# Encoder layer (gated DeltaNet and short convolution) in fp32: roots on GpSimd, merge copies kept on one engine, the second norm scaled ahead of a plain transposition, queries without the learned tokens

## The chip, the cores and the metric

The kernel runs on one core of a Trainium2 chip. The metric is the device time of one execution in microseconds, the median of several runs. Each profile is of one execution. The engines are called as the profile calls them: PE is TensorE (PEld its weight loads), DVE is VectorE, ACT is ScalarE, POOL is GpSimd, and SP is the engine that issues most of the DMAs.

## The reference

One encoder layer works on 1024 rows of 1024 columns with 16 learned tokens ahead of them. Cut to what matters:

```python
h = rmsnorm(h_res, norm1_w)                     # x * rsqrt(mean(x*x) + 1e-6) * w
q, k, v, z, b_raw, a_raw, sc_b, sc_c, sc_x, gate_a, gate_b = split(h @ w_in)
# branch A, 8 heads of 128: centred convolution of q|k|v over 5 rows, SiLU, l2norm of q and k,
#   gated delta rule in chunks of 64 rows, forward and backward, o = o_fwd + o_bwd
#   per chunk: triangular solve with (I + strict lower part of beta * k k^T * decay)
#   o = o * rsqrt(mean(o*o) + 1e-6) * norm_w * silu(z)
# branch B: sc_b * convolution over 3 rows of (sc_c * sc_x)
merged = sigmoid(gate_a) * (o_dn @ w_branch_dn) + sigmoid(gate_b) * (y_b @ w_branch_sc)
h_res += merged @ w_out
gu = rmsnorm(h_res, norm2_w) @ w_gate_up        # 1024 x 5632
h_res += (silu(gu[:, :2816]) * gu[:, 2816:]) @ w_down
out = rmsnorm(h_res, final_norm_w)[16:]
```

All of it is float32. The rows of the learned tokens matter for k, v and the gates, since later rows attend to them; the output leaves these rows out.

## The kernel before

**Products.** Every large product is split for precision: each operand into a high part in the matmul format fp32r and a low part that is the rest, and three matmuls add up (high by high, low by high, high by low: lines 293, 294 and 295 in stage 1, 1269 to 1271 in the output projection, 1329 to 1331 in part two). A split is a cast on ACT and a subtraction on DVE (lines 86 and 87, 889 and 886, 988 and 991).

**Start (0 to 23 us).** Nine row tiles, the first with the 16 learned tokens ahead, come in groups of 1, 2, 3 and 3 (loop at line 948). ACT squares a tile and sums it (L957). DVE makes 1/rms of the whole group: a mean (L958), then `rsqrt` (L127 to L141), an integer shift and a magic constant for a first guess, and three Newton steps. L979 multiplies a tile by 1/rms and by the weight row w1row, PE transposes it (L83), and L988 and L991 split it. POOL sets up masks and identities meanwhile, lines 1020 to 1051. Here the compiler's scheduler sets the order of each engine.

**Stage 1 (23 to 1057 us).** PE works through dense units: for each of the 8 heads k, q and v (`u_qkv`, i = 0, 1, 2), and the short convolution's and the gates' columns. A unit has three chunks of columns (QCH: 336, 320 and 384 of the 1040 rows) of 24 matmuls each. Heads are worked on between them, each as a stream: `g_norm` (squares, k by k, the decayed matrices PQ and NP), `g_inv` (the inverse of the triangular matrix, by blocks of 16 merged to 32, 64 and 128), and `g_scan` (the chunked recurrence, then the norm of o and its transposition). The order is written by hand: each stream is a generator that yields a due time, clocks T for pe, dve, act and pool are moved on by `on`, `pe`, `A` and `V` with planned costs, and whichever is due goes next, with dense matmuls as filling. Jobs for DVE (`conv_job`, `norm_job`, `norm`) are queued in lanes and taken one instruction at a time. An engine keeps strictly to the order in which this plan emits. POOL carries the decay tables of the next heads on short rows (L609 to L619), some of which wait for a DMA.

**Merges.** In `g_inv`, the step from 32 to 64 multiplies small blocks into two PSUM banks, pp and px (L672 to L674). Four blocks of pp go to NP by copies on ACT and DVE in turn (L679 and L676), then one block of px to X64 on each (L681 on DVE, L682 on ACT); X64 is part of the tile XT. The next matmuls (L689, L690) read both. The step from 64 to 128 copies one half on ACT (L699) and one on DVE (L700).

**Norm of o.** `g_scan` ends with a job on DVE: the root of nine columns, then eight instructions that scale one chunk of o each; after it PE transposes four chunks at a time.

**Second norm (1300 to 1412 us).** The output projection goes row tile by row tile. DVE adds the residual (L1272) and multiplies by the weight row (L1277), ACT squares (L146), DVE makes 1/rms (L147, L126 to L135). One tile later `norm_T` makes diag(1/rms) (L158) and lets PE multiply the tile by it, in full fp32 (L166, eight products of 128 by 128), which scales and transposes together. The last tile's norm_T comes behind the first product of part two. The scheduler sets the order.

**Part two and the tail (1412 to 2032 us).** The gate and up columns go through a Strassen scheme, then the down projection adds into rows; `finish` scales a row tile by the final norm (L1489 to L1497). Of the last four tiles half is squared ahead of time; when the last half has come, it is squared (L1490), joined (L1491), the root is taken (L126 to L135), and both halves are scaled on ACT (L1494) and DVE (L1496) and stored.

Of the kernel before, what the change touches and what calls it, by code (L numbers as in the profile page):

```python
# [10 lines left out]
I32 = mybir.dt.int32  # L11
# [26 lines left out]
def encoder_layer(ctx: ExitStack, tc: tile.TileContext, x, meta, norm1_w, w_in,  # L38
# [84 lines left out]
    def rsqrt(y, a, tmp):  # L123
        column = y.shape[-1] == 1
        if column:
            nc.vector.tensor_scalar(out=tmp, in0=a, scalar1=-0.5, scalar2=None, op0=ALU.mult)  # L126
        nc.vector.tensor_scalar(out=y.bitcast(I32), in0=a.bitcast(I32), scalar1=1, scalar2=None,  # L127
                                op0=ALU.logical_shift_right)
        nc.vector.tensor_scalar(out=y.bitcast(I32), in0=y.bitcast(I32), scalar1=-1,
                                scalar2=0x5F3759DF, op0=ALU.mult, op1=ALU.add)  # L130
        if column:

            for _ in range(3):
                nc.vector.scalar_tensor_tensor(out=a, in0=y, scalar=tmp, in1=y, op0=ALU.mult, op1=ALU.mult)
                nc.vector.scalar_tensor_tensor(out=y, in0=a, scalar=1.5, in1=y, op0=ALU.add, op1=ALU.mult)  # L135
            return
        for _ in range(3):
            nc.vector.tensor_tensor(out=tmp, in0=y, in1=y, op=ALU.mult)
            nc.vector.scalar_tensor_tensor(out=tmp, in0=tmp, scalar=-0.5, in1=a,
                                           op0=ALU.mult, op1=ALU.mult)  # L140
            nc.vector.scalar_tensor_tensor(out=y, in0=tmp, scalar=1.5, in1=y,  # L141
                                           op0=ALU.add, op1=ALU.mult)

    def rms_scale(pool, src, p, tag, junk):
        ss = pool.tile([P, 3], F32, tag=tag, name=uid(tag), bufs=3)
        nc.scalar.activation(junk[:p], src, AF.Square, accum_out=ss[:p, 0:1])  # L146
        nc.vector.tensor_scalar(out=ss[:p, 0:1], in0=ss[:p, 0:1], scalar1=1.0 / D, scalar2=EPS,  # L147
                                op0=ALU.mult, op1=ALU.add)
        rsqrt(ss[:p, 1:2], ss[:p, 0:1], ss[:p, 2:3])
        return ss[:p, 1:2]  # L150
# [4 lines left out]
    def norm_T(t, rs, hn):  # L155

        diag = tp.tile([P, P], F32, tag="diag", name=uid("diag"), bufs=1)
        nc.vector.tensor_scalar(out=diag, in0=ident, scalar1=rs, scalar2=None, op0=ALU.mult)  # L158
        c = slice(t % 4 * P, t % 4 * P + P)
        pts = []  # L160
        for g in range(2):
            pt = psany().rearrange("p (k t) -> p k t", k=4)
            pts.append(pt)
            for k in range(4):
                kk = 4 * g + k
                mm(pt[:, k], hn[:, kk * P:(kk + 1) * P], diag, start=True, stop=True)  # L166
# [47 lines left out]
    QCH = ((0, 336), (336, 320), (656, 384))  # L214

# [93 lines left out]
    def conv_job(raw, dst, col, st_, key):  # L309

        for h0, hn in HALF:
# [16 lines left out]
    def u_qkv(h, i, w):  # L328
# [9 lines left out]
        for ci, (t0, n) in enumerate(QCH):  # L338
            po = psm()
            yield from dense_steps(po, w, hx, t0, n)  # L340
            if raw is None:
                raw = row_buffer()
                nc.gpsimd.memset(raw[:, 0:2], 0.0)
# [6 lines left out]
            if ci == 1:  # L350
                job = enqueue("conv", conv_job(raw, dst, col, sub, "t"))
                raws.append(job)
# [103 lines left out]
    def norm_job(st_, ssk1, cc, ce, he, y, tmp, sk):  # L456
        nc.vector.tensor_tensor(out=ce, in0=cc, in1=he, op=ALU.mult)
        V(18)
        yield T["dve"] + DEP
        rsqrt(y, ssk1, tmp)  # L460
        [V(9) for _ in range(11)]
# [28 lines left out]
    def g_norm(h, st_):  # L490
# [5 lines left out]
        ssk, ssq, rk2, ssk1, y, tmp, sk = (small[:, :, i] for i in range(7))  # L496
# [51 lines left out]
        nc.vector.tensor_scalar(out=ssk1, in0=ssk, scalar1=EPS, scalar2=None, op0=ALU.add)  # L548
        nc.vector.reciprocal(rk2, ssk1)
# [4 lines left out]
        on("dve", 500)  # L554
# [20 lines left out]
        enqueue("norm", norm_job(st_, ssk1, cc, ce, he, y, tmp, sk))  # L575

    def g_inv(h, st_):
# [96 lines left out]
        for i, (d, a, b, Xs, xo) in enumerate(pairs):  # L674
            if i % 2:
# [878 lines left out]
```

## Time and profile before

| | us |
|---|---|
| three runs | 2034.18, 2039.75, 2039.87 |
| median | 2039.75 |
| the profiled execution, its own time | 2033.3 |
| its span | 2031.6 |
| ACT busy in the span | 791.9 |

The span is the stretch from the first to the last instruction of the core, and 1.7 us of the execution lie around it. A row of a timeline gives the start in us, the duration, the engine, the line, the operation, what it writes and reads, the shape, how many instructions in a row it stands for, and in brackets how long the engine was idle just before and what ended that. A row of windows gives the stretch, its length, and for PE, PEld, DVE, ACT and POOL the busy time with the number of instructions, then PE's granted clock, the busy share of the DMA engines and GB/s. A row of the waits has the waiting line, the line that released it, and the total, the number and the longest of the waits.

### The profile page before, as it was taken

Reading aid. Unit: us, or ns where it says so; the run is one execution under the profiler, and the core shown is the slowest. Engines: PE = TensorE matmul, PEld = TensorE weight load, DVE = VectorE, ACT = ScalarE, POOL = GpSimd, SP = SyncE. Lnnn points to the kernel's source line nnn. Section 1 sums busy time; section 2 is a strip of 40 time slices with the busy share of each in tenths; the row PEclk is TensorE's granted clock in tenths of the full one; section 3 lists DMA queues with packets and bytes.
Section 4 is the critical chain, followed back from the end, with each engine's and each line's share of the span. In section 5 each row is a group of like instructions: output and inputs, shape, how many; then the busy total and the mean of one; then the engine's idle time right before and its main releaser. Section 6 shows DMA issues by size and latency. Waiting matters only on the chain.

```text
span 2031.6 us, 32113 instructions
## 1 busy us (share of the span) xinstructions
PE 1982.7 (98%) x12075; PEld 1732.7 (85%) x12075; DVE 1412.6 (70%) x3129; ACT 791.9 (39%) x1873; POOL 108.0 (5%) x394
## 2 busy tenths in 40 slices
PE   6999999999999999999999999999999999999998
PEld 6899998999999888988888888888888888878886
DVE  6789586887887797857245534458988777756576
ACT  5363235364544554453334211124323222224343
POOL 1002110202020201101000000000000000000000
PEclk9999999999999999999999999999999999999999
DMA  4122322222222223232327743122766345477654
GB/s 141 39 88 68 74 60 63 78 63 57 75 58 84 59 79 84 71 92 79 99 63 233 233 135 115 52 98 84 254 225 220 129 167 172 159 267 248 195 176 156
DMA packets 250723, 248.40 MB, mean 122 GB/s; under 512 B 46085, under 2 KB 190774, under 8 KB 248134
## 3 DMA queue, kind: packets, MB, share of 16 engines
q1 hardware_dynamic: 250565, 246.34, 38.9%
q8 instruction: 95, 1.56, 0.3%
q14 instruction: 63, 0.51, 0.1%
HBM read 179.62 MB, written 66.67 MB: 121 GB/s over the span
## 4 chain that ended last, share of the span: by engine, by line
PE 80%; DVE 11%; ACT 3%; DMA 2%; issue 1%; SPq 0%; POOL 0%; DVEq 0%; ACTq 0%; POOLq 0%
PE pm L293 9%; PE pm L295 9%; PE pm L294 9%; PE pm L1330 3%; PE pm L1331 3%; PE pm L1329 3%; PE pd L1330 2%; PE pd L1331 2%; PE pd L1329 2%; DVE kq L316 2%; PE pe L1331 2%; PE pe L1330 2%; PE pe L1329 2%; PE pd L121 1%; PE pd L120 1%
## 5 line engine op out<-in xcount | busy, mean ns | idle before, releaser
L293 PE MATMUL pm<-hTh,wh 128*128 128x384 f32 (+4 forms) x1424 | 525.9, 369 | 3.5 <-issue 1.3
L295 PE MATMUL pm<-hTh,wl 128*128 128x384 f32 (+4 forms) x1424 | 490.4, 344 | 0.4 <-issue 0.2
L294 PE MATMUL pm<-al,wh 128*128 128x384 f32 (+4 forms) x1424 | 488.8, 343 | 0.3 <-DVE al L991 0.3
L295 PEld LDWEIGHTS pm<-hTh,wl 128*128 128x128 f32 x1424 | 267.6, 188 | 20.6 <-issue 0.5
L293 PEld LDWEIGHTS pm<-hTh,wh 128*128 128x128 f32 x1424 | 268.8, 189 | 19.2 <-ACT wh L889 1.4
L294 PEld LDWEIGHTS pm<-al,wh 128*128 128x128 f32 x1424 | 269.0, 189 | 17.1 <-issue 1.4
L87 DVE TENSOR_TENSOR al<-raw,ring_h 128x1024 fp32r<-128x1024 f32 x73 | 88.5, 1223 | 65.3 <-ACT ring_h L86 64.7
L886 DVE TENSOR_TENSOR wl<-raw,wh 128x512 fp32r<-128x512 f32 x134 | 90.6, 688 | 52.9 <-ACT wh L889 52.5
L86 ACT CAST ring_h<-raw 128x1024 fp32r<-128x1024 f32 x73 | 76.7, 1054 | 106.3 <-PE pe L1474 37.5
L316 DVE SCALAR_TENSOR_TENSOR kq<-ra,wc,kq 128x520 f32<-128x520 f32 x128 | 97.3, 760 | 3.8 <-ACT kq L346 2.4
L86 ACT CAST wh<-raw 128x1024 fp32r<-128x1024 f32 x45 | 47.4, 1053 | 122.8 <-issue 30.0
L771 ACT ACTIVATE w<-pd,small 128x128 f32<-128x128 f32 x128 | 40.1, 365 | 111.0 <-PE pd L764 102.7
L889 ACT CAST wh<-raw 128x512 fp32r<-128x512 f32 x134 | 78.7, 618 | 9.7 <-PE pm L294 9.6
L452 DVE TENSOR_TENSOR fP<-fP,tm 128x135 f32<-128x135 f32 (+23 forms) x248 | 71.4, 288 | 5.0
L448 DVE TENSOR_TENSOR tm<-fP,fN 128x135 f32<-128x135 f32 (+23 forms) x248 | 71.5, 288 | 4.3
L1333 DVE TENSOR_TENSOR b<-pm,b 128x512 f32<-128x512 f32 x67 | 45.1, 687 | 33.2 <-PE pm L1331 31.0
L793 DVE SCALAR_TENSOR_TENSOR S<-S,eGl,pd 128x128 f32<-128x128 f32 x104 | 31.8, 344 | 49.7 <-PE pd L781 26.6
L87 DVE TENSOR_TENSOR wl<-raw,wh 128x1024 fp32r<-128x1024 f32 x45 | 54.9, 1219 | 11.5 <-ACT wh L86 11.3
L617 POOL TENSOR_TENSOR tm<-mP,mN 1x15 f32<-1x15 f32 (+7 forms) x120 | 40.9, 341 | 261.7 <-DMA mN<-ndm 253.3
L1333 DVE TENSOR_TENSOR b<-pd,b 128x512 f32<-128x512 f32 x54 | 36.5, 686 | 22.3 <-PE pd L1331 22.3
L486 ACT ACTIVATE PQ<-PQ,negG 128x128 f32<-128x128 f32 x128 | 43.4, 393 | 15.6 <-DVE PQ L481 15.5
L316 DVE SCALAR_TENSOR_TENSOR vT<-ra,wc,vT 128x520 f32<-128x520 f32 x64 | 48.2, 753 | 1.7 <-ACT vT L346 0.6
(624 smaller groups left out, 4623.4 us busy)
## 6 DMA issues: line engine op xcount, KB each, us to landing
raw<-in_w_in_dram SPq DMA_DIRECT2D x72, 512.0 KB
raw<-in_w_gate_up_dram SPq DMA_DIRECT2D x44, 512.0 KB
sums<-in_w_down_dram SPq DMA_DIRECT2D x22, 512.0 KB
t_d<-sums SPq DMA_DIRECT2D x11, 1024.0 KB
raw<-s_d SPq DMA_DIRECT2D x44, 256.0 KB
raw<-t_d SPq DMA_DIRECT2D x44, 256.0 KB
act_d<-b SPq DMA_DIRECT2D x43, 256.0 KB
raw<-act_d SPq DMA_DIRECT2D x33, 256.0 KB
```

Source lines behind the costliest of these rows:

```text
L86: nc.scalar.copy(hi, src)
L87: nc.vector.tensor_tensor(out=lo, in0=src, in1=hi.bitcast(F32), op=ALU.subtract)
L293: mm(po[:, :n], wh[:, k], xh[:, k, t0:t0 + n], start=(k == 0), stop=False)
L294: mm(po[:, :n], wh[:, k], xl[k][:, t0:t0 + n], start=False, stop=False)
L295: mm(po[:, :n], wl[:, k], xh[:, k, t0:t0 + n], start=False, stop=(k == KT - 1))
L316: nc.vector.scalar_tensor_tensor(out=acc, in0=raw[:, h0 + t:h0 + t + hn], scalar=wc[:, t, col:col + 1], in1=acc, op0=ALU.mult, op1=ALU.add)
L886: nc.vector.tensor_tensor(out=u[1][1][:, k], in0=u[2][:, k], in1=u[1][0][:, k].bitcast(F32), op=ALU.subtract)
L889: nc.scalar.copy(u[1][0][:, k], u[2][:, k])
L1329: mm(po, ah[:, k], bhk, start=k == 0, stop=False)
L1330: mm(po, ah[:, k], blk, start=False, stop=False)
L1331: mm(po, al[:, k], bhk, start=False, stop=k == 3)
L1333: add = lambda out, a, b: nc.vector.tensor_tensor(out=out, in0=a, in1=b, op=ALU.add)
```

## The change

1. `rsqrt` becomes one POOL instruction, a tensor power by −0.5 with a constant tile `minus_half`, with an optional add of D · EPS ahead of it. The division by D goes into the weight rows, which are multiplied by the root of D once: w1row on POOL, the rows of the second and the final norm on ACT.
2. In the second norm the seven first tiles are multiplied by 1/rms and weight row in one DVE instruction, and PE transposes them plainly (L83). The last tile keeps diag.
3. The query units take columns 14 to 335 in the first chunk instead of 0 to 335; their convolution begins at column 16, and one memset is dropped.
4. In the merges the four copies to NP are all on ACT, both copies to X64 on DVE, and both copies of the last step on ACT.
5. In `g_norm` the root is issued right behind its operand instead of in `norm_job`; in `g_scan` the eight scalings of o move from DVE to ACT, four ahead of each four transpositions. Planned costs change with both.

```diff
-    def rsqrt(y, a, tmp):
...
+    minus_half = keep.tile([P, 9], F32, name="minus_half")
+    nc.gpsimd.memset(minus_half, -0.5)
+
+    def rsqrt(y, a, plus=None):
+        if plus is not None:
+            nc.gpsimd.tensor_scalar(out=y, in0=a, scalar1=plus, scalar2=None, op0=ALU.add)
+            a = y
+        nc.gpsimd.tensor_tensor(out=y, in0=a, in1=minus_half[:a.shape[0], :a.shape[1]], op=ALU.pow)
...
     def norm_T(t, rs, hn):
-        diag = tp.tile([P, P], F32, tag="diag", name=uid("diag"), bufs=1)
-        nc.vector.tensor_scalar(out=diag, in0=ident, scalar1=rs, scalar2=None, op0=ALU.mult)
+        if t == KT - 1:
+            diag = tp.tile([P, P], F32, tag="diag", name=uid("diag"), bufs=1)
+            nc.vector.tensor_scalar(out=diag, in0=ident, scalar1=rs, scalar2=None, op0=ALU.mult)
...
-                mm(pt[:, k], hn[:, kk * P:(kk + 1) * P], diag, start=True, stop=True)
+                if t == KT - 1:
+                    mm(pt[:, k], hn[:, kk * P:(kk + 1) * P], diag, start=True, stop=True)
+                else:
+                    transpose(pt[:, k], hn[:, kk * P:(kk + 1) * P])
...
+    QUERY = ((14, 322), *QCH[1:])
...
-        for ci, (t0, n) in enumerate(QCH):
+        for ci, (t0, n) in enumerate(QUERY if i == 1 else QCH):
...
+        rsqrt(y, ssk1)
...
-        on("dve", 500)
+        on("dve", 950)
...
-        for i, (d, a, b, Xs, xo) in enumerate(pairs):
-            if i % 2:
-                nc.vector.tensor_copy(NP[B(a), :, d, B(b)], pp[B(a)])
-                on("dve", 460)
-            else:
-                nc.scalar.copy(NP[B(a), :, d, B(b)], pp[B(a)])
-                A(256)
+        for d, a, b, Xs, xo in pairs:
+            nc.scalar.copy(NP[B(a), :, d, B(b)], pp[B(a)])
+            A(128)
         nc.vector.tensor_copy(X64[B(1), :, 0:32], px[B(1)])
-        nc.scalar.copy(X64[B(2), :, 32:64], px[B(2)])
-        yield max(on("dve", 450), A(256))
+        nc.vector.tensor_copy(X64[B(2), :, 32:64], px[B(2)])
+        yield max(on("dve", 920), T["act"] + HOP)
...
-        nc.vector.tensor_copy(NP[hi, :, 1, lo], pp[hi])
-        yield max(on("dve", 710), A(512))
+        A(512)
+        nc.scalar.copy(NP[hi, :, 1, lo], pp[hi])
+        yield A(512) + HOP
...
-            for c in range(NC):
-                nc.vector.tensor_scalar(out=oacc[c], in0=oacc[c], scalar1=y[:, c:c + 1], scalar2=None, op0=ALU.mult)
-                V(P, 2)
-                yield T["dve"] + DEP
...
-        yield T["dve"] + HOP
+        yield T["dve"] + 1500
...
+            for c in range(4):
+                nc.scalar.activation(oacc[4 * c4 + c], oacc[4 * c4 + c], AF.Copy, scale=y[:, 4 * c4 + c:4 * c4 + c + 1])
+                t = A(P)
+            yield t
...
+                    nc.gpsimd.tensor_scalar(out=w1row, in0=w1row, scalar1=ROOT, scalar2=None, op0=ALU.mult)
...
+    nc.scalar.mul(wrow, wrow, ROOT)
...
-            nc.vector.tensor_tensor(out=hn, in0=xr, in1=wrow, op=ALU.mult)
+            nc.vector.scalar_tensor_tensor(out=hn, in0=xr, scalar=rs, in1=wrow, op0=ALU.mult, op1=ALU.mult)
...
+    nc.scalar.mul(wfr, wfr, ROOT)
```

How the instructions stand on POOL at the start, before (Uf, Ub, Ef, Eb, U2f, U2b, mask are masks, BA the store of the gates):

```order
masks.py:199 AFFINE_SELECT ident<-ident 128x128
L1022 AFFINE_SELECT Uf<-Uf 128x128
L1020 MEMSET Ub 128x128
L1020 MEMSET Ef 128x128
L1022 AFFINE_SELECT Ub<-Ub 128x128
L1022 AFFINE_SELECT Ef<-Ef 128x128
L1020 MEMSET Eb 128x128
L1028 MEMSET ones 128x128
L1022 AFFINE_SELECT Eb<-Eb 128x128
L1033 TENSOR_SCALAR U2f<-Uf 64x128
L1035 COPY U2f<-Uf 64x128
L1033 TENSOR_SCALAR U2b<-Ub 64x128
```

And after the change (ss_145 is the sum of squares of the first tile, ss_171 that of the next two):

```order
masks.py:199 AFFINE_SELECT ident<-ident 128x128
L944 TENSOR_SCALAR w1row<-w1row 128x1024
L128 TENSOR_SCALAR ss_145<-ss_145 128x1
L1012 AFFINE_SELECT Uf<-Uf 128x128
L130 TENSOR_TENSOR ss_145<-ss_145,minus_half 128x1
L1010 MEMSET Ub 128x128
...
L1028 TENSOR_SCALAR mask_605<-Ub 128x128
L1041 MEMSET BA 128x288
L128 TENSOR_SCALAR ss_171<-ss_171 128x2
L130 TENSOR_TENSOR ss_171<-ss_171,minus_half 128x2
```

The scaling of the weight row and the first root stand among the masks, the second group's root behind all of them.

DVE at the start, before (L979 normalizes a tile, L991 and L87 split):

```order
L979 SCALAR_TENSOR_TENSOR xr_144<-xr_144,ss_143,w1row 128x1024
L958 TENSOR_SCALAR ss_176<-ss_176 128x2
L127 TENSOR_SCALAR ss_176<-ss_176 128x2
L129 TENSOR_SCALAR ss_176<-ss_176 128x2
L991 TENSOR_TENSOR al_121<-pm_161,hTh 128x4x128
L991 TENSOR_TENSOR al_122<-pm_168,hTh 128x2x128
L991 TENSOR_TENSOR al_123<-pm_168,hTh 128x2x128
L138 TENSOR_TENSOR ss_176<-ss_176 128x2
L87 TENSOR_TENSOR wl_200<-raw_197,wh_199 128x1024
...
L141 SCALAR_TENSOR_TENSOR ss_176<-ss_176 128x2
L979 SCALAR_TENSOR_TENSOR xr_177<-xr_177,ss_176,w1row 128x1024
L979 SCALAR_TENSOR_TENSOR xr_181<-xr_181,ss_176,w1row 128x1024
```

And after (L969 is the normalizing line now, L981 the split of a tile):

```order
L969 SCALAR_TENSOR_TENSOR xr_146<-xr_146,ss_145,w1row 128x1024
L969 SCALAR_TENSOR_TENSOR xr_172<-xr_172,ss_171,w1row 128x1024
L981 TENSOR_TENSOR al_123<-pm_156,hTh 128x4x128
L87 TENSOR_TENSOR wl_185<-raw_182,wh_184 128x1024
L981 TENSOR_TENSOR al_124<-pm_163,hTh 128x2x128
L981 TENSOR_TENSOR al_125<-pm_163,hTh 128x2x128
L981 TENSOR_TENSOR al_123<-pe_199,hTh 128x4x128
L981 TENSOR_TENSOR al_124<-pe_206,hTh 128x2x128
L981 TENSOR_TENSOR al_125<-pe_206,hTh 128x2x128
L969 SCALAR_TENSOR_TENSOR xr_176<-xr_176,ss_171,w1row 128x1024
```

The chains of the root are gone, and the second tile's normalizing (xr_172) has moved ahead of the splits of the first tile and of the first weight.

DVE behind the last tile of the second norm, before (ss_2353_14742 is that tile's root; the other rows split and add for part two):

```order
L134 SCALAR_TENSOR_TENSOR ss_2353_14742<-ss_2353_14742 128x1
L87 TENSOR_TENSOR b_2366_14840<-al_14054,b_2366_14840 128x4x384
L135 SCALAR_TENSOR_TENSOR ss_2353_14742<-ss_2353_14742 128x1
L87 TENSOR_TENSOR mA_14829<-al_14053,mA_14829 128x4x384
L134 SCALAR_TENSOR_TENSOR ss_2353_14742<-ss_2353_14742 128x1
L153 TENSOR_TENSOR al_14053<-b_hl,al_14053 128x4x384
L135 SCALAR_TENSOR_TENSOR ss_2353_14742<-ss_2353_14742 128x1
L1333 TENSOR_TENSOR b_2365_14839<-pm_14861,b_2365_14839 128x512
L185 TENSOR_TENSOR al_14053<-al_14053,b_hl 128x4x384
L1333 TENSOR_TENSOR b_2365_14839<-pm_14898,b_2365_14839 128x512
L158 TENSOR_SCALAR diag_14913<-ident,ss_2353_14742 128x128
L87 TENSOR_TENSOR wl_14937<-raw_14938,wh_14936 128x1024
```

And after, where the root is on POOL:

```order
L1268 TENSOR_TENSOR s_2345_14469<-s_2342_14414,w_2275_13846 128x1024
L141 TENSOR_TENSOR al_13850<-al_13850,b_hl 128x4x128
L141 TENSOR_TENSOR al_13852<-al_13850,pd_14476 128x4x128
L141 TENSOR_TENSOR al_13851<-al_13850 128x4x128
L87 TENSOR_TENSOR wl_14597<-raw_14598,wh_14596 128x1024
L147 TENSOR_SCALAR diag_14633<-ident,ss_2347_14472 128x128
L87 TENSOR_TENSOR w_2385_14693<-raw_14540,w_2385_14693 128x512
L87 TENSOR_TENSOR b_2361_14562<-al_13850,b_2361_14562 128x4x384
L87 TENSOR_TENSOR mA_14549<-al_13851,mA_14549 128x4x384
```

diag has moved up ahead of the splits of part two's operands.

61 lines of the change are left out of this document (19 added, 42 removed).

## The prediction

> **What bounds the kernel now.** I read the page's busy table first, then the windows cut at the borders of the stages, then the waits of TensorE, then the timelines at the two ends.
>
> ```profile
> span 2031.6 us, 32113 instructions
> PE 1982.7 (98%) x12075; PEld 1732.7 (85%) x12075; DVE 1412.6 (70%) x3129; ACT 791.9 (39%) x1873; POOL 108.0 (5%) x394
> ```
>
> TensorE is busy 98% of the span. The windows (length, then each engine's busy time, with the granted clock) say where the other 49 us are.
>
> ```profile
> 0.00:22.90 22.90, 6.30 (x28) 5.35 (x28) 12.67 (x39) 13.39 (x26) 5.12 (x27) 1.00 0.94 287
> 22.90:1057.00 1034.10, 1014.71 (x7741) 930.14 (x7742) 757.83 (x2109) 474.74 (x1468) 102.84 (x367) 1.00 0.25 70
> 1300.00:1412.00 112.00, 110.16 (x549) 92.89 (x548) 73.87 (x166) 39.40 (x61) 0.00 (x0) 1.00 0.28 91
> 1412.00:2022.00 610.00, 608.54 (x2683) 503.03 (x2681) 451.15 (x653) 205.18 (x248) 0.00 (x0) 1.00 0.59 197
> 2022.00:2031.60 9.60, 0.02 (x1) 0.00 (x0) 4.33 (x17) 2.17 (x4) 0.00 (x0) 0.65 0.40 149
> ```
>
> So idle time lies in four places: 16.6 us at the start, 19.4 in stage 1 (22.9 to 1057), 1.8 beside the second norm, 9.6 in the tail. Only two kinds of edit can pay: less TensorE work, or a shorter wait in one of those places. An engine made lighter elsewhere pays nothing. Stage 1's larger waits from 50 us on (in total, times, longest):
>
> ```profile
> PE pe L542 <- DVE PQ L571: 5.1, 4, 3.3
> PE pd L689 <- DVE XT L681: 2.8, 2, 2.6
> PE pe L83 <- DVE Nm L525: 2.1, 2, 1.2
> ```
>
> All three wait for VectorE, 10.0 us together.
>
> **Second norm: less TensorE work.** The timeline of TensorE shows a scaled transposition of one tile, and plain ones at the start of the kernel, with matmuls of 336 columns ahead of them:
>
> ```profile
> 1347.36 1.95 PE L166 MATMUL pm<-diag,s 128*128 128x128 f32 x16
> 1349.06 0.48 PE L1269 MATMUL pe<-b,wh 128*128 128x512 f32 x1
> ...
> 27.83 0.32 PE L1010 MATMUL pe<-hTh,wba 128*64 128x336 f32 x1
> 28.75 0.32 PE L1010 MATMUL pe<-hTh,wba 128*64 128x336 f32 x1
> 28.91 0.60 PE L83 MATMUL pd<-ident,xr 128*128 128x128 f32 x4
> 29.34 1.47 PE L83 MATMUL pm<-ident,xr 128*128 128x128 f32 x12
> 30.65 0.60 PE L83 MATMUL pe<-ident,xr 128*128 128x128 f32 x4
> ```
>
> The eight fp32 products with diag are sixteen passes: 1349.06 − 1347.36 = 1.70 us, 106 ns a pass. A plain transposition is one pass: 1.31 us for twelve, 109 ns. Seven tiles change: 7 × (1.70 − 8 × 0.109) = −5.8 us. On a saturated engine all of it counts. The multiplication by 1/rms moves into the VectorE instruction that multiplies by the weight row, and transposition comes a tile later, so the longer wait of hn for its root is covered; uncovered, it would cost about a root per tile, 7 × 0.3 us.
>
> The Trainium skill, in "TensorE: Matmul & The Clock Gate", Part 4 on the PE-mode transpose, speaks against this: it says that one transposition took about 275 ns in a kernel and that the clock gate doesn't count it as busy. By that price eight would cost 2.2 us instead of 1.70, +3.5 us for seven tiles. The rows above decide against it: twelve at 109 ns in a window with a granted clock of 1.00.
>
> **Queries: less TensorE work.** The first chunk of each of eight query units loses 14 of 336 columns in its 24 matmuls. Between 27.83 and 28.75 lie six steps: 153 ns for 336 columns, 0.46 ns a column, so 192 × 14 × 0.46 = −1.2 us (nothing, if a step had a fixed part only; the 14 columns can't cost more). The dropped memsets and the shorter first half of the convolution lie on engines that aren't waited for there.
>
> **The last tile's diag.** For the eighth tile diag stays, but its root no longer threads through VectorE's queue:
>
> ```profile
> 1387.34 0.19 ACT L146 ACTIVATION_READ_ACCUMULATOR s<-s 128x1 f32 x1
> ...
> 1400.32 0.27 DVE L158 TENSOR_SCALAR diag<-ident,ss 128x128 f32<-128x128 f32 x1
> ...
> 1400.65 2.05 PE L166 MATMUL pe<-diag,s 128*128 128x128 f32 x16 [1.50 <-DVE diag L158]
> ```
>
> The sum of squares is there at 1387.5, but diag only 13 us later, since its nine small operations alternate with long splits in VectorE's order. In the new order diag stands right behind one split of the next weight. TensorE's 1.50 us go: −1.5 (0 if another operand of part 2 is late next).
>
> **Tail.** VectorE and ScalarE after TensorE's last matmul at 2022.0:
>
> ```profile
> 2022.70 0.75 DVE L1496 SCALAR_TENSOR_TENSOR mA<-mA,ss,w 128x512 f32<-128x512 f32 x1
> 2023.37 0.68 DVE L1333 TENSOR_TENSOR mA<-pe,mA 128x512 f32<-128x512 f32 x1
> ...
> 2025.18 0.16 DVE L1491 SCALAR_TENSOR_TENSOR ss<-ss,sq 128x1 f32<-128x1 f32 x1 [1.13 <-ACT b L1490]
> ...
> 2027.16 0.72 ACT L1494 ACTIVATE b<-b,ss 128x512 f32<-128x512 f32 x1 [2.01 <-DVE ss L135]
> ```
>
> The root's ten operations take 1.98 us of this path. Two GpSimd operations replace them. The trace has no power; GpSimd's nearest row is the product of two short rows:
>
> ```profile
> L617 POOL TENSOR_TENSOR tm<-mP,mN 1x15 f32<-1x15 f32 (+7 forms) x120 | 40.9, 341 | 261.7 <-DMA mN<-ndm 253.3
> ```
>
> At 0.34 us each, with a handover from and to another engine, I take 0.9 us: −1.1. VectorE is also free for the last sum L1333 earlier, since the chain of the tile ahead (to 2022.70) is off it: −1.1. Together −2.2, between −2.7 and 0 (a power of 1.3 us more).
>
> **Start.** Here GpSimd comes onto the path.
>
> ```profile
> 1.83 0.21 POOL L1020 MEMSET Ub<- 128x128 f32 x1
> ...
> 5.07 0.30 POOL L1038 TENSOR_SCALAR mask<-Uf 128x128 f32<-128x128 f32 x1
> ...
> 5.77 0.34 POOL L1051 MEMSET BA<- 128x288 f32 x1
> ...
> 8.33 1.06 ACT L957 ACTIVATE jk<-xr 128x1024 f32<-128x1024 f32 x1 [1.37 <-DMA xr<-in_x_dram]
> ...
> 8.97 1.28 DVE L979 SCALAR_TENSOR_TENSOR xr<-xr,ss,w1row 128x1024 f32<-128x1024 f32 x1
> ...
> 12.10 0.69 DVE L991 TENSOR_TENSOR al<-pm,hTh 128x512 fp32r<-128x512 f32 x1 [0.64 <-ACT hTh L988]
> ...
> 13.89 1.23 DVE L87 TENSOR_TENSOR wl<-raw,wh 128x1024 fp32r<-128x1024 f32 x1
> ...
> 16.81 2.48 DVE L979 SCALAR_TENSOR_TENSOR xr<-xr,ss,w1row 128x1024 f32<-128x1024 f32 x2
> 18.24 1.94 PE L83 MATMUL pe<-ident,xr 128*128 128x128 f32 x8 [5.52 <-DVE xr L979]
> ...
> 22.02 0.42 PE L293 MATMUL pm<-hTh,wh 128*128 128x336 f32 x1 [0.42 <-ACT hTh L988]
> ```
>
> In the new order GpSimd waits for the weight row's DMA, scales it, and only then takes the first root. That DMA was issued ahead of the transfer that the square at 8.33 waited for, so 8.3 is its latest; I take 7.1. The scaling has 1024 elements a partition; eight times the mask of 128 (0.30 us with its fixed part) would be 2.4 us, and two memsets of 512 about 1 us; I take 1.7. Behind it come the two operations of the root at 0.34 us and a handover: the first hn near 10.0 instead of 8.97. The mask set-up, from 1.83 to 6.11 on an idle engine before, now stands between the first root and the second: 10.0 + 4.3, plus the root, is hn1 at about 15.0. That beats 16.81, because VectorE's chain of eleven operations is gone. But VectorE's order has hn1 second now, so the splits of the first tile and of the first weight (12.10 to 15.12, 3.0 us) queue behind it: hn2 starts at 15.0 + 1.3 + 3.0 = 19.3 and ends at 20.6, where it ended at 19.29. The first dense matmul came 2.7 us behind that end, at 22.02; now at about 23.3: +1.3. Transpositions that were moved ahead of the second unit's first chunk wait for later squares; of one square, 1.06 us, I put half in the way: +0.6. Sum +1.9, from +0.5 (scaling at 1 us, the dense start set by DMAs that are busy 94% of this window) to +6 (scaling at 2.4 us, each mask operation slowed by the traffic).
>
> **Stage 1.** Order and due times are planned by hand, and the planner's clocks change, so the fill is laid anew everywhere. One merge of before:
>
> ```profile
> 668.49 0.42 DVE L676 COPY NP<-pd 32x256 f32<-32x256 f32 x1 [0.71 <-ACT NP L679]
> 668.94 0.36 ACT L679 COPY NP<-pd 32x256 f32<-32x256 f32 x1 [0.49 <-DVE NP L676]
> 669.34 0.43 DVE L676 COPY NP<-pd 32x256 f32<-32x256 f32 x1 [0.43 <-ACT NP L679]
> ...
> 670.25 0.36 ACT L682 COPY XT<-pd 32x256 f32<-32x256 f32 x1 [0.94 <-DVE XT L681]
> ...
> 670.36 0.30 PE L689 MATMUL pd<-XT,NP 64*64 64x64 f32 x2 [2.55 <-DVE XT L681]
> ```
>
> Copies into one tile take turns across engines, each at about 0.42 us with its handover, and the DVE and ACT copies to XT queue behind them. From 668.1 to 670.36 are 2.2 us; four ACT copies in a row of 0.36 with XT beside them on VectorE are 1.4. So a merge is 0.8 us shorter, and of the 2.55 us wait 0.8 goes. VectorE loses about 34 operations a head (two root chains, eight scalings, copies), 7 us at the 0.2 us that a link of the tail's chain takes, so PQ (3.3 us late once) should not be late: −3.3 − 0.8 = −4, against an end of −10 (all three waits go). The other end is +4: eight heads each find a new half microsecond, since ScalarE gets eight scalings ahead of transpositions, and the root's plan of 1.5 us may be short. On GpSimd's queue the new roots stand among memsets that wait; in the printed order each root follows the wait that ends earlier than it, so I cost that at nothing.
>
> **Sum.** −5.8 − 1.2 − 1.5 − 2.2 + 1.9 − 4 = −12.8 us. The profiled execution took 2033.3 us (span 2031.6), so it would be about 2020.5. The three runs are 2039.75, 2039.87 and 2034.18: the profiled one is like the lowest, and the median lies 6.45 above it. On the median the forecast is 2039.75 − 12.8 = 2027.0 us.
>
> **Rivals.**
> *The power is slow (slower).* No row shows its price. Each of eight heads waits for a root between the last square and the scalings; the plan leaves 1.5 us. Beyond that each microsecond costs about 1 × 8 heads, 3 at the start, 1 in the tail: 12 us. So it turns the sum at 1.5 + 12.8 / 12 = 2.6 us for 9 columns; at 4 us the time is 2039.75 − 12.8 + 12 × 2.5 = 2057. For it: the operation is not an elementary product, and 0.34 us is the mean of another. Against it: nine elements a partition. 13%. The Trainium skill's "GPSIMD Engine Reference", engine selection, gives elementwise work to VectorE, with GpSimd about half as fast on two inputs; no row here shows the same shape on both.
> *Stage 1 gives nothing and the start costs +6 (same).* −5.8 − 1.2 − 1.5 − 2.2 + 6 = −4.7, 2035. For it: 98% busy leaves little, and a new layout makes new waits. 17%.
> *The norms of stage 1 pay in full (faster, more).* −12.8 − 6 is 2021. 10%, inside faster.
>
> My forecast has 60%. What a measurement of this kernel can tell from no change is about 0.3%, 6.1 us. Faster by more: 60 + 10, 0.70; within: 0.17; slower: 0.13. The range takes in the bounds: low, all gains at their ends, a start of +0.5 and the run-to-run step, 2014; high, the second rival with stage 1 at +4, 2039. What is outside is most of the slow power and a remainder below.
>
> **What would show it.** Right: the eight transpositions of a tile in 0.87 us, diag for the last tile before 1393 on the old clock, no wait of 1.5 us before it, the last root 0.9 us after L1490, a dense start near 23.3. Wrong: a power of over 2 us in GpSimd's rows, a wait of the heads' scalings for it, a dense start past 26, or TensorE idle in stage 1 of 19 us or more.

## The result and the profile after

The changed kernel takes 2015.2 us (median of four runs, 2014.96 to 2015.98). Beside it the kernel before ran once more, in 2033.16 us, so that its median over four runs is 2036.97 us. The ratio is 0.9895, with a 95% interval of 0.9874 to 0.9916: about 21 us faster, where 12.8 us were forecast. The profiled execution took 2014.96 us, and its span is 2013.2 us, 18.4 us less than before's.

Part of the distance between 21 and 18.4 lies in the base. Three later sets of 13 runs of the kernel before have medians of 2034.56, 2034.09 and 2036.19 us, so the 2039.75 of the first three runs was some 4 to 6 us high. From here on spans and stages are compared.

The windows of the changed kernel, cut at the first dense matmul, one fixed matmul of the branch projections, the output projection and part two, show where the 18.4 us come from.

```profile
0.00:25.05 25.05, 6.13 (x27) 5.10 (x27) 7.79 (x13) 11.51 (x22) 10.53 (x32) 1.00 0.84 262
25.05:1103.30 1078.25, 1069.57 (x7998) 978.64 (x7998) 736.20 (x1884) 523.35 (x1581) 133.31 (x380) 1.00 0.28 78
...
1288.30:1370.70 82.40, 82.40 (x394) 68.84 (x392) 39.56 (x53) 22.91 (x40) 6.06 (x14) 1.00 0.33 109
1370.70:1805.00 434.30, 432.50 (x1916) 357.93 (x1914) 346.50 (x486) 136.32 (x173) 1.08 (x2) 1.00 0.56 188
```

The same cuts in the kernel before:

```profile
0.00:22.02 22.02, 5.73 (x27) 5.11 (x27) 11.79 (x37) 12.51 (x25) 5.12 (x27) 1.00 0.97 295
22.02:1113.50 1091.48, 1071.78 (x7998) 977.20 (x7999) 787.79 (x2162) 496.12 (x1500) 102.84 (x367) 1.00 0.27 77
...
1298.40:1387.10 88.70, 88.70 (x449) 75.48 (x449) 50.45 (x131) 23.79 (x41) 0.00 (x0) 1.00 0.30 101
1387.10:1821.20 434.10, 432.25 (x1915) 357.68 (x1914) 347.05 (x495) 135.27 (x171) 0.00 (x0) 1.00 0.56 188
```

| stage | forecast | measured, after minus before |
|---|---|---|
| start, to the first dense matmul | +1.9 | 25.05 − 22.02 = +3.0 |
| stage 1, with the queries' columns | −4 − 1.2 | 1078.25 − 1091.48 = −13.2 |
| second norm, transposition | −5.8 | 82.40 − 88.70 = −6.3 |
| part two, with the last diag | −1.5 | 434.30 − 434.10 = +0.2 |
| branch and down projections | 0 | +0.5 |
| tail, from TensorE's last matmul | −2.2 | (2013.2 − 2006.2) − (2031.6 − 2022.0) = −2.6 |

Stage 1 holds the larger part of the 18.4 us, and all that the forecast missed: −13.2 where −5.2 stood. TensorE is idle in it for 1078.25 − 1069.57 = 8.7 us, where it was 1091.48 − 1071.78 = 19.7 us. The waits of TensorE in stage 1 after the change no longer have PQ, XT or Nm among them; the four largest are:

```profile
PE pe L1103 <- DVE gc L1097: 2.0, 1, 2.0
PE pe L83 <- ACT jk L495: 1.8, 1, 1.8
PE pd L753 <- DVE r L748: 1.4, 4, 0.8
PE pm L286 <- ACT wh L879: 1.1, 1, 1.1
```

### The profile page after: what moved, and what is told of

It is laid out like the page before. It is cut to its first block, busy times and chain, and to the rows that moved or that the text cites. A ratio compares the mean times of both kernels' runs of the same rounds, so it can differ in the third digit from the quotient of the medians.

```text
span 2013.2 us, 31690 instructions
## 1 busy us (share of the span) xinstructions
PE 1974.9 (98%) x12019; PEld 1728.0 (86%) x12019; DVE 1334.9 (66%) x2660; ACT 818.9 (41%) x1955; POOL 159.1 (8%) x444
## 4 chain that ended last, share of the span: by engine, by line
PE 92%; DVE 3%; DMA 1%; ACT 1%; issue 0%; SPq 0%; POOLq 0%; POOL 0%; ACTq 0%; DVEq 0%
PE pm L286 12%; PE pm L288 12%; PE pm L287 11%; PE pm L1320 3%; PE pm L1322 3%; PE pm L1321 3%; PE pd L1322 3%; PE pd L1321 3%; PE pd L1320 3%; PE pe L1322 2%; PE pe L1321 2%; PE pe L1320 2%; PE pd L753 2%; PE pe L533 1%; PE pd L120 1%; PE pd L121 1%
## 5 line engine op out<-in xcount | busy, mean ns | idle before, releaser
L87 DVE TENSOR_TENSOR al<-raw,ring_h 128x1024 fp32r<-128x1024 f32 x73 | 88.3, 1224 | 65.7 <-ACT ring_h L86 65.3
L309 DVE SCALAR_TENSOR_TENSOR kq<-ra,wc,kq 128x520 f32<-128x520 f32 (+1 forms) x128 | 96.5, 754 | 6.0 <-ACT kq L340 4.9
L128 POOL TENSOR_SCALAR ss<-ss 128x1 f32<-128x1 f32 (+2 forms) x16 | 5.0, 316 | 944.4 <-ACT b L1476 605.6
L130 POOL TENSOR_TENSOR small<-small,minus_half 128x9 f32<-128x9 f32 x16 | 29.0, 1811 | 465.7 <-DVE small L817 269.3
L87 DVE TENSOR_TENSOR wl<-raw,wh 128x1024 fp32r<-128x1024 f32 x45 | 54.9, 1220 | 11.8 <-ACT wh L86 11.8
```

The source lines that it names most:

```text
L87: nc.vector.tensor_tensor(out=lo, in0=src, in1=hi.bitcast(F32), op=ALU.subtract)
L309: nc.vector.scalar_tensor_tensor(out=acc, in0=raw[:, h0 + t:h0 + t + hn], scalar=wc[:, t, col:col + 1], in1=acc, op0=ALU.mult, op1=ALU.add)
```

## Experiments: the parts one by one

Theories: **V**, the change made VectorE's queue in stage 1 shorter, and so its waits went. **M**, the merges did it. **L**, the waits belong to the order that the planner happened to lay, and any new order deals them anew. Each kernel below is the kernel before with one part of the change. For stage 1 one measure serves all kernels: the idle time of TensorE between 50 and 1050 us of the span, 1000 minus its busy time in that window. It is 18.3 us before and 7.5 us after.

```profile
50.00:1050.00 1000.00, 981.74 (x7520) 899.66 (x7520) 734.72 (x2050) 457.67 (x1428) 102.84 (x367) 1.00 0.26 72
```

And after the change:

```profile
50.00:1050.00 1000.00, 992.45 (x7607) 912.28 (x7605) 697.86 (x1837) 491.97 (x1531) 131.07 (x376) 1.00 0.26 72
```

The expectations speak of the idle time of all of stage 1, 19.7 and 8.7 us, which adds the ends. Both measures see only the stretches in which TensorE does nothing; what slows it while it counts as busy shows in the length of the stage alone.

**Stage 1's roots on GpSimd and o's scalings on ScalarE alone.**

```diff
-        rsqrt(y, ssk1, tmp)
-        [V(9) for _ in range(11)]
...
+        power(y, ssk1)            # right behind ssk1, in g_norm
...
-                nc.vector.tensor_scalar(out=oacc[c], in0=oacc[c], scalar1=y[:, c:c + 1], ...)
+                nc.scalar.activation(oacc[4 * c4 + c], oacc[4 * c4 + c], AF.Copy, scale=...)
```

> The kernel before, with only stage 1's roots as powers on GpSimd and the eight scalings of o on ScalarE (with their planned costs). Theory V (the gain of stage 1 comes from VectorE's queue, which loses two root chains and eight scalings a head): TensorE idle between the first dense matmul and the first branch projection falls from 19.7 us to 8 to 12, the kernel is 8 to 11 us faster. Theory M (the merges' copies made VectorE late): idle stays at 15 or more, at most 3 us faster. Theory L (the waits depend on how the hand-made plan happens to fall, no part pays alone): idle moves by some us either way and doesn't add up with the other parts. A second power of 1.8 us for nine columns should be seen twice a head.

2021.3 us, ratio 0.9931 (0.9914 to 0.9948); idle 7.8 us, 9.1 in all of stage 1. Theory V's number for the idle time; the gain in time, some 13 us, is above all that was expected.

**The merges' copies alone.**

```diff
-        for i, (d, a, b, Xs, xo) in enumerate(pairs):
-            if i % 2:
-                nc.vector.tensor_copy(NP[B(a), :, d, B(b)], pp[B(a)])
...
+        for d, a, b, Xs, xo in pairs:
+            nc.scalar.copy(NP[B(a), :, d, B(b)], pp[B(a)])
```

> The kernel before, with only the merges' copies kept on one engine each. Theory V: one or two of the 2.55 us waits go, idle of stage 1 from 19.7 to 16 or 17, 2 to 3 us faster. Theory M: idle falls to 8 to 12, 8 to 11 us faster. Theory L: moves by some us either way.

2022.14 us, ratio 0.9931 (0.9916 to 0.9946); idle 9.9 us, 11.1 in all of stage 1. Theory M's number, from another part. The parts' gains, 10.5 and 8.3 us of idle time, don't add up, since both together with the rest give 10.7. That fits L, but two parts that take away the same waits would not add up either.

**The queries' columns alone.**

```diff
+    QUERY = ((14, 322), *QCH[1:])
...
-        for ci, (t0, n) in enumerate(QCH):
+        for ci, (t0, n) in enumerate(QUERY if i == 1 else QCH):
```

> The kernel before, with only the shorter first chunk and convolution of the eight query units. All theories: 1.1 to 1.2 us less busy TensorE time. V and M: idle of stage 1 unchanged within 1 us, so the kernel 1 us faster, which is within 0.3%. L: idle moves by several us although no wait is touched.

2022.4 us, ratio 0.9939 (0.9922 to 0.9955); idle 10.6 us. This part touches none of the waits, and saves 1.2 us of matmuls. It gained 12 us. V and M fall as the only cause, since neither allowed more than 1 us here.

**The second norm alone.**

```diff
-                mm(pt[:, k], hn[:, kk * P:(kk + 1) * P], diag, start=True, stop=True)
+                if t == KT - 1:
+                    mm(pt[:, k], hn[:, kk * P:(kk + 1) * P], diag, start=True, stop=True)
+                else:
+                    transpose(pt[:, k], hn[:, kk * P:(kk + 1) * P])
```

> The kernel before, with only the second norm's seven tiles scaled on VectorE and transposed plainly; roots stay on VectorE. Seven tiles at 0.87 instead of 1.70 us: 5.8 us faster from the first output projection to part two, and the wait of 1.50 us for the last tile's diag stays, since its chain stays. If the root chain ahead of the scaling delayed the transpositions, TensorE would wait at L83 there, up to 2 us a tile, and the gain would go. If the single-pass transposition cost 275 ns, 3.5 us slower.

2028.05 us, ratio 0.9974 (0.9961 to 0.9986), 5.3 us. From the first output projection to part two it takes 82.3 us (1305.5 to 1387.8), where the kernel before takes 88.7. The wait for the last tile's diag, which was expected to stay at 1.50 us, is 0.6 us here. Stage 1, whose order this part leaves alone, keeps 17.8 us of idle time.

## Experiments: order against work

The order can be parted from the work, since the planner takes its sizes as arguments. First a nudge of the planner's clock, with all work as before:

```diff
-            yield from dense_steps(po, w, hx, t0, n)
+            yield from dense_steps(po, w, hx, t0, n, n - 14 if i == 1 and ci == 0 else None)
```

> The kernel before with all its work and every instruction as it was; only the planner is told 322 columns instead of 336 for the first chunk of the eight query units, so its clock for TensorE runs 0.14 us less a unit and the hand-made plan falls otherwise. Theory V or M (a part's own saving took the waits away): idle of stage 1 stays near 19.7 us, time within 0.1% of before. Theory L (the waits are accidents of how the plan fell, and any nudge deals them anew): idle falls to 9 to 13 us as in the three parts, 7 to 11 us faster, though nothing was saved.

2033.53 us, ratio 0.9996 (0.9987 to 1.0006); idle 15.8 us, 17.0 in all of stage 1. L's number was missed, and the time is what V and M expected: the wait of 3.3 us for PQ stayed in this order, that of 2.5 us for XT shrank to 0.4, and smaller ones came. So not every nudge helps. The next two settle the query part: one has its order, instruction for instruction on TensorE, VectorE and ScalarE, with before's sizes; the other has before's order with the small sizes.

```diff
-            pe(3 * (n / 2.4 + 13))
+            pe(3 * ((pn or n) / 2.4 + 13))     # n is computed, pn is planned
...
-                V(hn, 1)
+                V(pn, 1)
```

> The order of the kernel with only the query part changed, on TensorE, VectorE and ScalarE instruction for instruction, but with the work of the kernel before: the queries compute all 336 columns and the convolution all 520 of its first half, only the planner is given the smaller sizes. If the saved columns took the waits away (V): idle of stage 1 near 19.7 us, time as before. If the order did it (L): idle 11 to 13 us as with the part, 7 to 9 us faster than before, 1 us slower than the part.

> The reverse: the order of the kernel before, but the queries compute 322 columns and convolve from column 16, and the planner is given the old sizes. If the saved columns took the waits away (V): idle 11 to 13 us, 8 to 10 us faster. If the order did it (L): idle 18 to 20 us, 1 us faster than before for 1.2 us less of matmuls.

The part's order with before's work: 2023.19 us, ratio 0.9941 (0.9925 to 0.9957).

```profile
50.00:1050.00 1000.00, 989.36 (x7578) 909.12 (x7578) 738.92 (x2062) 460.24 (x1436) 101.02 (x367) 1.00 0.26 73
```

Before's order with the part's work: 2034.85 us, ratio 0.9994 (0.9984 to 1.0003).

```profile
50.00:1050.00 1000.00, 981.95 (x7518) 899.18 (x7517) 734.23 (x2050) 456.36 (x1428) 101.86 (x360) 1.00 0.26 72
```

The order alone brings the 12 us (idle 10.6 us); the work alone brings nothing that can be told (18.1 us). In all of stage 1 the idle time is 11.8 and 19.5 us, as L expected; the gain in time is above its 7 to 9 us. This parts order and work for the queries' columns only. Of the 12 us, 7.6 are idle time between 50 and 1050 us, while stage 1 as a whole is 10.6 us shorter (1091.48 against 1080.84), so some of the gain lies in time that counts as busy. What the order did can be read at one head. In the kernel before, where TensorE waits longest for PQ (3.34 us, at 334.46), VectorE and then TensorE:

```profile
329.21 3.21 DVE L316 SCALAR_TENSOR_TENSOR vT<-ra,wc,vT 128x520 f32<-128x520 f32 x4
332.33 0.17 DVE L548 TENSOR_SCALAR small<-small 128x9 f32<-128x9 f32 x1
...
333.89 0.42 DVE L571 TENSOR_TENSOR PQ<-pe,PQ 128x256 f32<-128x256 f32 x1
...
329.55 0.70 PE L542 MATMUL pe<-kq 128*128 128x256 f32 x2
329.89 0.50 PE L293 MATMUL pm<-hTh,wh 128*128 128x320 f32 x1
...
330.81 0.31 PE L295 MATMUL pm<-hTh,wl 128*128 128x320 f32 x1
334.46 0.67 PE L542 MATMUL pe<-kq 128*128 128x256 f32 x2 [3.34 <-DVE PQ L571]
```

And in the query part's order with before's work, at the same head:

```profile
331.65 0.75 DVE L318 SCALAR_TENSOR_TENSOR vT<-ra,wc,vT 128x520 f32<-128x520 f32 x1
332.33 0.17 DVE L551 TENSOR_SCALAR small<-small 128x9 f32<-128x9 f32 x1
...
336.15 0.41 DVE L574 TENSOR_TENSOR PQ<-pe,PQ 128x256 f32<-128x256 f32 x1
...
332.29 0.70 PE L545 MATMUL pe<-kq 128*128 128x256 f32 x2
332.63 0.52 PE L294 MATMUL pm<-hTh,wh 128*128 128x384 f32 x1
...
336.57 0.44 PE L294 MATMUL pm<-hTh,wh 128*128 128x384 f32 x1
...
337.20 0.59 PE L545 MATMUL pe<-kq 128*128 128x256 f32 x2
```

In both orders VectorE begins the short chain that ends with the awaited write of PQ at 332.33, behind a convolution instruction, and in the second the write ends later (336.56 instead of 334.31). VectorE isn't earlier; TensorE has other work. The rows of TensorE show the second and the third pair of products k by k of this head. Before, six dense matmuls stand between them, done at 331.1, and then TensorE waits for PQ. In the other order twelve dense matmuls, a merge and three more dense matmuls stand there, and the third pair comes at 337.20, when PQ is done. At this head the order decides how much filling TensorE has while VectorE works.

## Experiments: how much is the change's own

If the order decides, then a single pair of orders says little on what the change is worth in stage 1. So constants of the planner were moved in both kernels alike (HOP, the assumed delay between engines; DEP, the spacing of dependent instructions), and the changed kernel's queries were planned at their old size:

```diff
-    HOP, TOPE, DEP = 200, 370, 127
+    HOP, TOPE, DEP = 210, 370, 127     # or 190, 370, 127, or 200, 370, 120
```

> The kernel before with one constant of the planner changed, the assumed delay from engine to engine, 210 instead of 200 ns; all the work as it was. If most plans for this work leave little idle and the kernel before was unlucky: 9 to 14 us of idle. If the work of the kernel before makes VectorE late whatever the plan: 16 to 21 us.

> The changed kernel with all its work; only the planner is told 336 columns for the first chunk of the queries where 322 are computed. If the low idle of 8.7 us is the change's own merit: 8 to 10 us again, no difference. If it is an accident of this plan: idle 11 to 20 us, 2 to 10 us slower than the changed kernel.

> The kernel before with the planner's assumed delay between engines at 190 instead of 200 ns, work unchanged. If its plan was merely unlucky: idle of stage 1 at 11 to 14 us, as with 210 ns. If 20 us are usual for it: 17 to 21 us.

> The kernel before with the planner's spacing of dependent VectorE instructions at 120 instead of 127 ns, work unchanged. Unlucky plan: idle 11 to 14 us; usual: 17 to 21 us.

> The changed kernel with 190 ns. If the change itself is worth something in stage 1: idle 8 to 11 us, below the kernel before at 190 ns by 2 us or more. If its 8.7 us were luck: 11 to 14 us, no different from before at 190 ns.

> The changed kernel with 210 ns; the kernel before had 12.8 us of idle at 210 ns. Own merit: 8 to 11 us. Luck: 11 to 14 us.

> The changed kernel with the spacing at 120 instead of 127 ns. Own merit: idle 8 to 11 us, 2 us or more below the kernel before at 120 ns. Luck: 11 to 14 us, no different from it.

| order | idle 50 to 1050 us, kernel before | changed kernel | time before's work, us | changed, us |
|---|---|---|---|---|
| as written | 18.3 | 7.5 | 2036.97 | 2015.2 |
| HOP 210 | 11.4 | 7.5 | 2026.31 | 2014.71 |
| HOP 190 | 17.6 | 6.0 | 2034.22 | 2010.82 |
| DEP 120 | 10.6 | 11.5 | 2024.98 | 2019.44 |
| queries planned at the other size | 15.8 | 10.0 | 2033.53 | 2017.07 |
| order of the query part | 10.6 | | 2023.19 | |

The expectations go by all of stage 1. For the kernel before, HOP 210 leaves 12.8 us of idle time there and DEP 120 12.0, as for an unlucky plan; HOP 190 leaves 19.0, as usual for its work. For the changed kernel, HOP 190 leaves 7.1 and HOP 210 8.7, as for a merit of its own (7.1 is even below its range); DEP 120 leaves 12.6, as for luck, and the queries planned at their old size 11.1, at the edge of luck.

The times in the rows for HOP 190 and DEP 120, and the changed kernel's at HOP 210, are of one run each. The work of the kernel before falls into two kinds of order: three that keep the wait for PQ of 3.3 us, at 15.8 to 18.3 us, and three without it, at 10.6 to 11.4. The changed work lies between 6.0 and 11.5. The four pairs with like constants differ by 10.7, 3.9, 11.6 and −0.9 us, on the mean 6.3. So of the 10.7 us of idle time that the change took away, some 6 are what it is worth over these orders, and the rest is the bad order that it happened to leave. By the length of stage 1, from the first dense matmul to the same matmul of the branch projections, the pairs differ by 13.2, 6.8, 18.1 and 2.4 us, on the mean 10.1, so of the 13.2 us some 10 are its worth; this counts the shorter columns in, and what the idle time leaves out. With the stretches at half clock (see the last section) taken out, the mean is the same. With so few orders both means are uncertain by several us.

## Experiments: the root, the start, part two

**The heads' last root taken twice**, in the changed kernel:

```diff
             rsqrt(y, sso)
+            rsqrt(y, sso)
```

> The changed kernel with the final root of each of the eight heads taken twice (the same value, the second overwrites the first), so it is 1.8 us longer. If the heads wait for their root: 8 x 1.8 = 14 us slower. If other planned work covers it: under 2 us slower, and the rival of the slow power would have needed a far longer power in stage 1.

2021.15 us, ratio to the kernel before 0.9938 (0.9923 to 0.9953); the span is 2018.8 us, 5.6 more than the changed kernel's, for 8 × 1.81 = 14.5 us of added powers. The rows of the waits show where:

```profile
PE pd L83 <- ACT NP L833: 3.8, 6, 1.1
```

(L833 is in ScalarE's scaling.) Neither expectation holds: no wait of TensorE is put down to the first power, and about six tenths of the second are covered too, or half, if the stretches at half clock are taken out (one in this profile's stage 1, two in the changed kernel's; see the last section).

**The start mended.**

```diff
-                    nc.gpsimd.tensor_scalar(out=w1row, in0=w1row, scalar1=ROOT, ...)
...
-            rsqrt(ss[:, 1, :nt], ss[:, 0, :nt], D * EPS)
+            nc.gpsimd.tensor_scalar(out=ss[:, 1, :nt], in0=ss[:, 0, :nt], scalar1=1.0 / D, scalar2=EPS, op0=ALU.mult, op1=ALU.add)
+            rsqrt(ss[:, 1, :nt], ss[:, 1, :nt])
```

The masks' lines also move ahead of the loop over the tiles.

> The changed kernel with its start mended: the first norm's mean is taken in the root's first operation (times 1/D, plus EPS, one instruction as before), so the weight row isn't scaled on GpSimd, and the masks are written ahead of the tiles. First root near 8.4 us instead of 10.8, the second near 12 instead of 17, the first dense matmul near 18 to 20 instead of 25.05: 5 to 7 us faster than the changed kernel, if the GpSimd queue is what held the start. If the weights' transfers hold it: first dense matmul not before 22, under 3 us faster. Stage 1 may shift by some us, since the scheduler there is a fixed plan but its start isn't.

2009.18 us, ratio to the kernel before 0.9879 (0.9864 to 0.9894); span 2007.5 us, 5.7 less than the changed kernel's. The timeline of the changed kernel's start:

```profile
7.06 2.81 POOL L944 TENSOR_SCALAR w1row<-w1row 128x1024 f32<-128x1024 f32 x1 [5.42 <-DMA w1row<-in_norm_w_dram]
...
10.27 0.57 POOL L130 TENSOR_TENSOR ss<-ss,minus_half 128x1 f32<-128x1 f32 x1
...
16.29 0.74 POOL L130 TENSOR_TENSOR ss<-ss,minus_half 128x2 f32<-128x2 f32 x1
17.06 1.28 DVE L969 SCALAR_TENSOR_TENSOR xr<-xr,ss,w1row 128x1024 f32<-128x1024 f32 x1 [4.90 <-POOL ss L130]
...
25.05 0.65 PE L286 MATMUL pm<-hTh,wh 128*128 128x336 f32 x1
```

And of the mended one:

```profile
7.11 0.56 POOL L130 TENSOR_TENSOR ss<-ss,minus_half 128x1 f32<-128x1 f32 x1
...
11.65 0.71 POOL L130 TENSOR_TENSOR ss<-ss,minus_half 128x2 f32<-128x2 f32 x1
...
17.80 0.65 PE L286 MATMUL pm<-hTh,wh 128*128 128x336 f32 x1
```

GpSimd's queue held the start, not the transfers; which of the two edits did more, no run tells. The first dense matmul comes 7.2 us earlier than in the changed kernel, and 4.2 earlier than before.

**Part two: the last tile's transpositions earlier**, on top of the mended start:

```diff
+    norm_T(*late_norm)
     ahead.append(part1(stationary1(1), sm[:, 1], sm[:, 3]))
-    norm_T(*late_norm)
```

> The changed kernel with the mended start, and with the last tile's transpositions of the second norm issued one product pair earlier in part two, since the new root has diag ready by then. TensorE's waits of 0.41 and 1.40 us for ScalarE's casts in part two should go: 1.5 us faster than with the mended start alone. If diag isn't ready at that place, a wait at the transpositions takes their place and nothing is gained.

2007.44 us, ratio 0.9865 (0.9847 to 0.9884), the fastest kernel here; the gain over the mended start, 1.7 us, is inside the intervals. The wait that it was to remove is still there, so the expectation of its mechanism failed:

```profile
1379.26 0.50 PE L1319 MATMUL pm<-b,mB 128*128 128x512 f32 x1 [1.44 <-ACT b L86]
```

In the profile of the mended start alone TensorE's clock is halved for 3.4 us right behind that wait, in this one it isn't; by the last section that is 1.7 us between the two profiles, whose spans differ by 2.3. So the gain can't be put down to the edit.

## Why the prediction was right or wrong

The direction and the places were right; the size was not, and the step that failed is stage 1's, "−3.3 − 0.8 = −4". It measured −11 of idle time, and −13.2 of length with the columns. It took the waits for PQ and XT as a matter of VectorE's load and of the merge's copies, and priced the relief by the longest of them. The load itself was forecast well: VectorE is busy 787.79 − 736.20 = 51.6 us less in stage 1, 6.4 a head, where 7 were taken. But a wait depends also on what the order gives TensorE to do meanwhile. For the queries' columns this is shown: before's order kept its waits with less work, and another order lost them with all the work. For the roots and the merges order and work were not parted. Over four pairs of plans the changed work is better by 6 us of idle time or 10 of length, so its lighter load may well help on the mean; that is not shown apart from the order.

The text said that "the fill is laid anew everywhere", and counted new waits as a cost of up to +4; that a new order could also undo a bad old one, it allowed only in the bound (all three waits go, −10) and in the third rival (10%). That bound is what came. Part of it was luck, in the old order and not in the new: three of six orders for the old work, and all five of the changed work's, are without the wait of 3.3 us. Even the means over the four pairs are more than the forecast. What a wait costs beyond its length, TensorE at half clock behind it (see the last section), the text put at nothing; in the two profiles it goes the other way, 1.7 us before and 3.4 after, so it doesn't explain the gain.

- Second norm: −5.8 forecast, −6.3 measured. Eight plain transpositions take 0.79 us (1310.96 to 1311.75), 99 ns each from start to start. The Trainium skill ("TensorE: Matmul & The Clock Gate", Part 4: PE-mode transpose) gives about 275 ns for one in a kernel. The trace agrees for the duration of a single one, 273 ns in the median of 24 on L83, but they overlap, and in a row the price is the 99 ns.

```profile
1310.96 1.03 PE L83 MATMUL pm<-ident,s 128*128 128x128 f32 x8
1311.75 0.48 PE L1260 MATMUL pe<-b,wh 128*128 128x512 f32 x1
```

- Queries' columns: −1.2 forecast; not resolved. The two pairs that differ by the columns alone differ by −0.8 us (2022.4 and 2023.19) and by −0.06% with an interval of −0.16 to +0.03%.
- The last diag: −1.5 forecast, +0.2 measured. The wait for diag did go: diag is ready at 1375.66, 6 us before TensorE uses it. But the bound "0 if another operand of part 2 is late next" came true: TensorE waits 0.41 and 1.40 us for ScalarE's casts of b.

```profile
1384.95 0.50 PE L1320 MATMUL pe<-b,mB 128*128 128x512 f32 x1 [0.41 <-ACT b L86]
1386.84 0.50 PE L1320 MATMUL pm<-b,mB 128*128 128x512 f32 x1 [1.40 <-ACT b L86]
```

- Tail: −2.2 forecast, −2.6 measured. From the end of the square, ScalarE now waits 1.07 us for the root instead of 2.01:

```profile
2007.83 0.29 POOL L128 TENSOR_SCALAR ss<-ss,sq 128x1 f32<-128x1 f32 x1 [2.45 <-ACT b L1481]
2008.21 0.57 POOL L130 TENSOR_TENSOR ss<-ss,minus_half 128x1 f32<-128x1 f32 x1
2008.81 0.72 ACT L1484 ACTIVATE b<-b,ss 128x512 f32<-128x512 f32 x1 [1.07 <-POOL ss L130]
```

- Start: +1.9 forecast, +3.0 measured. The mechanism was right (weight row, then root, then masks, then the second root); the scaling of the weight row was mis-sized, 2.81 us where 1.7 were taken and 2.4 was the bound, and the power too, 0.57 us where 0.34 was.
- The slow power: it is slow in part, 1.81 us for nine columns, more than the planned 1.5. The price "1 × 8 heads" a microsecond was too high: the doubled root cost 5.6 us for 14.5, so 0.4 of what was assumed, or half, with the clock taken out.

## What to carry to other kernels

Where an order is planned by hand and the main engine is 98% busy, a change of any planned cost can deal the waits anew; before a gain there is put down to the change, run the old work in the new order and the new work in the old one. At a wait, look at both sides: when the awaited engine is done, and what the waiting engine's order could have put in between. Price a change over a few nudged plans of both kernels, not over one. A helper that moves to an idle engine takes its place in that engine's queue, so look at what stands ahead of it: a set-up moved ahead, and a scaling folded into an operation that was there anyway, gained 5.7 us of span.

## What the runs showed of the hardware

GpSimd's tensor power, on 128 partitions, took 0.57 us for one column (one of 17 took 1.40), 0.74 for two and 1.81 for nine:

```profile
L130 POOL TENSOR_TENSOR small<-small,minus_half x16: 1803/1812/1815, 142.4 to 1040.7; 128x9 f32<-128x9 f32 x16
```

In these profiles TensorE's granted clock drops to 0.50 for 3.4 us at a time, at two places of one run for 6.8. In stage 1 this comes once before the change, behind the wait of 3.34 us, and twice after it, behind waits of 2.01 us (at 101.63) and 1.80 us (at 319.46). Before:

```profile
335.20:338.60 3.40, 3.40 (x38) 3.28 (x37) 2.40 (x6) 2.13 (x6) 0.00 (x0) 0.50 0.01 2
338.60:341.00 2.40, 2.40 (x15) 2.35 (x15) 1.93 (x6) 0.43 (x1) 0.00 (x0) 1.00 0.16 26
```

```profile
337.58 0.47 PE L295 MATMUL pm<-hTh,wl 128*128 128x320 f32 x1
337.85 0.47 PE L293 MATMUL pm<-hTh,wh 128*128 128x320 f32 x1
...
338.79 0.31 PE L294 MATMUL pm<-al,wh 128*128 128x320 f32 x1
338.93 0.30 PE L295 MATMUL pm<-hTh,wl 128*128 128x320 f32 x1
```

Matmuls of 320 columns come 0.27 us apart in the stretch and 0.14 behind it. Half of 3.4 us is lost, 1.7 us, and counts as busy. Not every such wait is followed by it: the kernel before waits 1.87 us until 97.31 and 2.55 us until 670.36 and keeps its clock, while the kernel with the second norm alone, in the same order of stage 1, loses it at both places. So runs of one kernel differ: that kernel took 2025.77 us at a mean granted clock of 0.997 and 2035.7 at 0.992. The later runs of the kernel before show clocks of 0.993 to 0.998, the changed kernel's four 0.997 and 0.998, so a few of the 21 us between the medians may be the clock's; no run parts them.

In the changed kernel the first dense matmuls of 336 columns came 0.28 us apart, and from 27.28 on 0.15 us apart, although the granted clock in this window is shown as 1.00; before the change they were 0.16 us apart from 23.18 on. TensorE had just been idle for 2.82 us there. The ratio is that of the half clock above, so a halved clock that the window doesn't show is likely, but not shown.

```profile
23.25 1.97 PE L83 MATMUL pd<-ident,xr 128*128 128x128 f32 x8 [2.82 <-DVE xr L969]
...
26.50 0.48 PE L286 MATMUL pm<-hTh,wh 128*128 128x336 f32 x1
26.78 0.48 PE L287 MATMUL pm<-al,wh 128*128 128x336 f32 x1
...
27.28 0.32 PE L286 MATMUL pm<-hTh,wh 128*128 128x336 f32 x1
27.43 0.32 PE L287 MATMUL pm<-al,wh 128*128 128x336 f32 x1
```
